# Making the rest of eight weight pieces by an adding transfer, in a hybrid decoder layer on one Trainium2 core

## The chip, the core and the metric

The kernel runs on one core of one Trainium2 chip. The metric is device time in microseconds (us): the median of the runs, beside one execution that was profiled. Five kinds of rows occur in the profile: PE is TensorE (PEld its weight loads), DVE is VectorE, ACT is ScalarE, POOL is GpSimd, SP is SyncE, which here only issues transfers. All transfers run on the core's 16 DMA engines.

## What is computed

The reference is one decoder layer in float32 with 256 tokens and a model width of 2048. Only its last line matters for the change:

```python
def swiglu(h, w_gu, w_down):
    gate, up = jnp.split(h @ w_gu, 2, axis=-1)
    return (jax.nn.silu(gate) * up) @ w_down

x = x + 0.5 * swiglu(rmsnorm(x, ffn1_norm[l]), ffn1_w_gu[l], ffn1_w_down[l])
# ... one input projection, sliding-window attention, HGRN2 recurrence, gated merge, output projection
x = x + 0.5 * swiglu(rmsnorm(x, ffn2_norm[l]), ffn2_w_gu[l], ffn2_w_down[l])
```

`w_gu` is 2048 x 11264 and `w_down` is 5632 x 2048, for either feed-forward part.

## The kernel before

**Two parts of every number.** The matrix products run in the type float32r, which keeps fewer bits than float32. So each operand is split: a first part `hi`, which is the value rounded to float32r, and a rest `lo`, which is the value less `hi`. A product of activations a and weights w is made of three: a_hi w_hi, a_hi w_lo and a_lo w_hi.

**Weights in pieces.** All weights stream from the chip's memory in 370 pieces of 1 MB (128 partitions x 2048 float32), in the order of their use; `plan` holds that order. `load_next` (line 128) issues the load of a piece into one of four buffers `w_raw`, on SP. `split_next` (line 141) makes the two parts: ACT copies `w_raw` into `w_hi`, rounding it (line 150, a CAST in the profile), and then DVE writes `w_raw - w_hi` into `w_lo` (line 151, a TENSOR_TENSOR). `w_hi` and `w_lo` have two buffers each, so the parts of piece i go where those of piece i-2 were. When `take` (line 157) hands out piece i, it issues loads up to piece i+4 and splits up to piece i+1.

**The products.** `project` (line 194) runs over the pieces of a projection. A piece holds two slices of 1024 columns (j = 0 and 1), each of two banks of 512. For each of the two token tiles and each j it issues six matmuls of 512 columns: bank 0 with hi, bank 0 with lo, bank 1 with hi, bank 1 with lo, then both banks with a_lo and hi. A piece so has 24 matmuls, of which the second is the first that reads `w_lo`. The first matmul that reads the columns 512 to 1023 of `w_lo` is the fourth, and for the next two quarters it is the eighth and the tenth.

**The second feed-forward part.** Counted from 0, the pieces 238 to 325 are those of `w_gu`: eleven groups of eight, a group being 512 gate and 512 up columns. After a group `ffn` applies silu and the product, and the result is transposed during the first two pieces of the next group: four transposes (`put_ps`) between its first and second piece, and four in the middle of the second, each followed by a CAST on ACT (`f_ah`) and a subtraction on DVE (`f_al`). The pieces 326 to 369 are those of `w_down`, 22 for either half of the columns.

**What sets the order.** The kernel is written as one sequence. The framework puts each engine's instructions in a list of its own, in an order that its scheduler chooses, and adds the waits on semaphores. Each engine runs its list in order. A transfer is issued by the engine in whose list it stands, and SP's loads are issued in order too.

Of the kernel before, what the change touches and what calls it, by code (L numbers as in the profile page):

```python
# [15 lines left out]
P = 128  # L16
D = 2048
S = 256
# [9 lines left out]
NEG = -3.0e38  # L28
# first column of each part of the input projection
C_Q, C_KV, C_GQ, C_GF, C_GI, C_GO, C_BR = 0, 1024, 1280, 2304, 3328, 4352, 5376  # L30
# places in the constants
# sums over the tokens of a chunk: from the reference, from the start, to the end, all of chunk 1 and 2
K_REF, K_HEAD, K_TAIL, K_ALL, K_SUMS = 0, 128, 256, 384, 388
K_MADD, K_TRIL, K_MLT, K_MUT, K_HM, K_INVF, K_END = 0, 128, 256, 384, 512, 640, 672
# 1 / (2 pi) in pieces of 12 bits
TURN_PIECES = 5


def turn_pieces():
    from fractions import Fraction  # L40
    import math

    # 1 / (2 pi) to 80 bits
    pi = Fraction(31415926535897932384626433832795028841971693993751, 10**49)
    rest = 1 / (2 * pi)
    out = []
    for _ in range(TURN_PIECES):
        e = math.floor(math.log2(float(rest))) - 11
        n = int(rest / Fraction(2) ** e)
        c = Fraction(n) * Fraction(2) ** e  # L50
        out.append(float(c))
        rest -= c
    return out
# [3 lines left out]
def tile_layer(  # L57
# [31 lines left out]

    # the last instruction of a kind, for others to be queued behind  # L90
    last = {}
# [3 lines left out]

# [1 line left out]
    ident = cp.tile([P, P], F32, name="ident")  # L97
# [9 lines left out]
    def load_gains(sources, c0, name):  # L107
        """vectors of P * n -> columns of gains from c0"""
        n = sum(src.shape[1] for src in sources) // P
        nat = s4(f"{name}_nat")[:n, :P]  # L110
        r = 0
        for src in sources:
            k = src.shape[1] // P
            nc.sync.dma_start(nat[r:r + k, :], src.rearrange("o (k p) -> (o k) p", p=P))
            r += k
        ps = trb(f"{name}_ps")
        transpose(ps[:, :n], nat)
        VE.tensor_copy(out=gains[:, c0:c0 + n], in_=ps[:, :n])
# [4 lines left out]

# [1 line left out]
    # The weights pass through in pieces of 1 MB, in the order of use: plan holds (name, parts), a part  # L125
    # being an access pattern and its columns in the piece.
    plan, loaded, ready = [], [], []
# [13 lines left out]
    def split_next():  # L141
        i = len(ready)
        if i < len(plan):
            raw = loaded[i]
            hi = wp.tile([P, 2048], F32R, name="w_hi", tag="hi")
            lo = wp.tile([P, 2048], F32R, name="w_lo", tag="lo")
            w = 1024 if i == 0 else 2048
            for c in range(0, 2048, w):
                c = slice(c, c + w)
                last["copy"] = SC.copy(hi[:, c], raw[:, c]).ins  # L150
                last["rest"] = VE.tensor_tensor(out=lo[:, c], in0=raw[:, c], in1=hi[:, c].bitcast(F32),  # L151
                                                op=ALU.subtract).ins
            ready.append((hi, lo))
# [12 lines left out]

    # Small work goes between the matrix products, half a piece apart.
    deferred, queues = [], []
# [25 lines left out]
    def project(name, ncols, nk, xh, xl, near_end=None):  # L194
        """(S, nk*128) @ the columns planned under name -> for each token tile its banks."""
        per = 2048 // ncols
# [4 lines left out]
        for kc in range(chunks):  # L201
            hi, lo = take(name)
            for t in range(T):
                tok = slice(t * P, (t + 1) * P)
                # the last piece bank by bank, so that they end one after the other
                order = [(range(per), [i]) for i in range(nb)] if kc == chunks - 1 else \
# [17 lines left out]
    class Normed:  # L224
        """x * gain, transposed, in two parts; the tokens' factors apart."""

# [12 lines left out]
        def add(self, q, pieces, kp):  # L239
            """columns q*512 + kp*256.. of both token tiles"""  # L240
            ps = trb(f"{self.name}_tp")
# [38 lines left out]
    class Parts:  # L280
        """transposed activations in two parts, four (128, S) tiles to a slot."""

# [10 lines left out]
        def put(self, k, n, ps, gain=None):  # L293
            """tiles k.. of a bank"""
            h, l = self.hi[k // 4], self.lo[k // 4]
# [11 lines left out]
    def put_transposed(parts, k0, nat, n, gain=None):  # L307
        """n column tiles of the token tiles nat[t] into tiles k0.. of parts"""
        for kp in range(n // 2):
            put_two(parts, k0, nat, kp, gain)  # L310
# [22 lines left out]
    def ffn(name, h, old, done):  # L333
        """done(q, pieces) takes columns q*512.. of old + ffn / 2"""
        act = Parts(f"{name}_act", 0)
# [42 lines left out]

# [1 line left out]
    wz = w_in[0]  # L380
# [8 lines left out]
    for cg in range(2):  # L389
        plan_project("po", w_out[0], cg * 1024, 1024, KT)  # L390
    plan_ffn("f2", ffn2_w_gu[0], ffn2_w_down[0])

# [1 line left out]
    xin = [[s4("xin")[:, :512] for t in range(T)] for q in range(4)]  # L394
# [15 lines left out]
    h1 = Normed("h1", "f1")  # L410
    # on both engines the activations come first
    a, v = h1.add(0, xin[0], 0)
# [5 lines left out]

    # small inputs
    pos_i = cp.tile([T, P], I32, name="pos_i")  # L420
# [13 lines left out]

    # rotary tables: gain * cos and gain * sin, tokens by 2 * 32 for queries and for keys
    rcos = cp.tile([P, T, 2, 2, 32], F32, name="rcos")
    rsin = cp.tile([P, T, 2, 2, 32], F32, name="rsin")

    def rotary_tables():
# [20 lines left out]
        def reduced(dst, src, big=1.5 * 2.0**23):  # L460
            """src less its nearest multiple of the unit at big"""
            VE.tensor_scalar(out=rd, in0=src, scalar1=big, scalar2=big, op0=ALU.add, op1=ALU.subtract)
            VE.tensor_tensor(out=dst, in0=src, in1=rd, op=ALU.subtract)
# [3 lines left out]
        for i, a in enumerate((a1.bitcast(F32), a2)):  # L467
            for j, c in enumerate(pieces):
                with tc.issue_after(last["rest"]):
                    VE.tensor_scalar(out=pr, in0=a, scalar1=c, scalar2=None, op0=ALU.mult)  # L470
                    if i == j == 0:
                        # up to 2**29: first less its multiple of 2**8
                        reduced(pr, pr, 1.5 * 2.0**31)
                    reduced(pr, pr)
                    VE.tensor_tensor(out=acc, in0=acc, in1=pr, op=ALU.add)
# [32 lines left out]

    # lower bound: the first row of the softmax over the table's two rows
    lbd = tc.dram_tile([2, HGW], F32, name="lbd")  # L510
# [29 lines left out]

# [1 line left out]
    rstd = h2.rstd  # L542
# [4 lines left out]
    def gated(name, bk):  # L547
        """silu of the banks"""
        res = []
# [18 lines left out]

# [1 line left out]
    lb, oml = s4("lb"), s4("oml")  # L570
# [10 lines left out]
    def forget():  # L581
        tiny = 2.0**-63
        for t in range(T):
# [7 lines left out]
            yield  # L591
            # log f over float32's range: f = max(f, c) * (min(f, c) / c)
            l = s4(f"logf{t}")
# [11 lines left out]
            yield  # L605
        # decay over the whole of chunks 1 and 2
        ps = trb("decay_ps")
# [15 lines left out]
    def hgrn():  # L623
        # q to the reference and to the chunk's start, k to the reference and to the chunk's end
        qs0 = [s4(f"q0{t}") for t in range(T)]
# [108 lines left out]

# [1 line left out]
    kv_bk = zproj("zkv", 256)  # L736
# [6 lines left out]
    def rotate(dst, src, t, which, nh, tmp):  # L743
        """dst, src, tmp: (P, nh, 64)"""
        c = lambda half: rcos[:, t, which, half, :].unsqueeze(1).broadcast_to([P, nh, 32])
# [11 lines left out]
    def attention():  # L757
# [25 lines left out]
        for t in range(T):  # L783
# [3 lines left out]
            VE.tensor_reduce(out=sc[:, t], in_=sq, axis=AX.X, op=ALU.add)  # L787
            # (mean + eps) ** -0.5 * HD ** -0.5
            VE.tensor_scalar(out=sc[:, t], in0=sc[:, t], scalar1=HD * EPS, scalar2=None, op0=ALU.add)
# [18 lines left out]
        def weigh(t, hq):  # L808
            """scores and their exponentials"""
            tok = slice(t * P, (t + 1) * P)  # L810
            g = hq // 2
            ss = t2("scores", (P, 4, P))
            # heads of one half of the partitions to a bank
            for e in range(2):
# [72 lines left out]

# [1 line left out]
    gA, gR = [], []  # L889
# [30 lines left out]

# [1 line left out]
    ffn("f2", h3, x2, keep(out))  # L922
# [8 lines left out]
def constants():  # L931
    """What depends on shapes alone."""
    import numpy as np
# [9 lines left out]
    sums[:, K_TAIL:K_TAIL + P] = same & (r > q)  # L943
    # per token tile two columns, for chunk 1 and for chunk 2
    sums[:, K_ALL + 0] = i >= 64
# [26 lines left out]
```

## Time and profile before

| | us |
|---|---|
| median of 3 runs | 2151.29 |
| lowest and highest | 2151.03, 2151.67 |
| span of the profiled execution, first to last instruction | 2149.6 |
| TensorE busy in it | 2139.2 |
| VectorE, ScalarE, GpSimd busy in it | 1067.7, 899.8, 14.8 |

The profiled execution has a span but no total of its own. It lies 1.7 us under the median of the runs, which is what the runs count around the first and the last instruction. A chain of waits follows the work back from the last instruction; a timeline lists one engine's instructions with start and duration.

### The profile page before, as it was taken

What the parts mean: (1) busy time and instruction counts of PE and PEld (TensorE: products, weight loads), DVE (VectorE), ACT (ScalarE), POOL (GpSimd) and SP (SyncE); (2) the same over time, 40 slices, a digit from 0 to 9 for tenths busy, and PEclk for the clock granted to TensorE, in tenths of its full rate; (3) what the DMA queues carried; (4) which work ended last, traced back from release to release, by engine and by line L of the source; (5) the groups of instructions that cost most, each with busy time, mean ns of one, the idle gap of its engine ahead of it and who ended that gap; (6) DMA issues with size and microseconds to landing.
All of it is one profiled execution on the core that took longest, in us unless ns stands there. A gap on an engine that the chain in (4) does not pass through costs nothing.

```text
span 2149.6 us, 23265 instructions
## 1 busy us (share of the span) xinstructions
PE 2139.2 (100%) x9775; PEld 1759.1 (82%) x9775; DVE 1067.7 (50%) x857; ACT 899.8 (42%) x757; POOL 14.8 (1%) x15
## 2 busy tenths in 40 slices
PE   8999999999999999999999999999999999999999
PEld 7888888888888888887777888888888888888887
DVE  4744444444444465445555565544444444444443
ACT  5543344333343354453455434444433343333332
POOL 0000000000000000000100000000000000000000
PEclk9999999999999999999999999999999999999999
DMA  7555555556565665554344555665555555565653
GB/s 275 187 195 179 194 192 184 192 192 213 194 221 189 212 208 176 178 174 137 128 164 139 186 177 189 212 201 191 196 179 194 194 183 190 191 215 192 222 198 118
DMA packets 159678, 405.87 MB, mean 189 GB/s; under 512 B 10243, under 2 KB 13014, under 8 KB 159574
## 3 DMA queue, kind: packets, MB, share of 16 engines
q1 hardware_dynamic: 156086, 398.10, 54.8%
q10 hardware_dynamic: 3488, 6.30, 0.8%
q8 instruction: 76, 1.25, 0.2%
q14 instruction: 28, 0.23, 0.0%
HBM read 398.06 MB, written 6.30 MB: 188 GB/s over the span
## 4 chain that ended last, share of the span: by engine, by line
PE 99%; DVE 0%; ACT 0%; DMA 0%; ACTq 0%; SPq 0%; issue 0%
PE f_gu L94 45%; PE f_d L94 22%; PE zbR L94 4%; PE zbA L94 4%; PE po L94 4%; PE zgo L94 2%; PE zgq L94 2%; PE zaq L94 2%; PE zgi L94 2%; PE pa L94 2%; PE zf L94 2%; PE pr L94 2%; PE put_ps L122 1%; PE o_ps L94 1%; PE s_ps L94 1%; PE zkv L94 1%
## 5 line engine op out<-in xcount | busy, mean ns | idle before, releaser
L151 DVE TENSOR_TENSOR w_lo<-w_raw,w_hi 128x2048 fp32r<-128x2048 f32 (+1 forms) x371 | 848.1, 2286 | 945.9 <-ACT w_hi L150 945.7
L150 ACT CAST w_hi<-w_raw 128x2048 fp32r<-128x2048 f32 (+1 forms) x371 | 707.3, 1907 | 1080.6 <-PE f_gu L94 501.7
L94 PE MATMUL f_gu<-w_hi,h_hi 128*128 128x512 f32 x1408 | 553.6, 394 | 2.0 <-ACT w_hi L150 2.0
L94 PE MATMUL f_gu<-w_lo,h_hi 128*128 128x512 f32 x1408 | 548.5, 390 | 0.0
L94 PE MATMUL f_gu<-w_hi,h_lo 128*128 128x512 f32 x1408 | 448.7, 390 | 0.0
L94 PEld LDWEIGHTS f_gu<-w_hi,h_hi 128*128 128x128 f32 x1408 | 265.0, 188 | 56.1 <-ACT w_hi L150 2.4
L94 PEld LDWEIGHTS f_gu<-w_hi,h_lo 128*128 128x128 f32 x1408 | 264.9, 188 | 56.0
L94 PEld LDWEIGHTS f_gu<-w_lo,h_hi 128*128 128x128 f32 x1408 | 265.0, 188 | 53.6
L94 PE MATMUL f_d<-w_hi,f_ah 128*128 128x512 f32 x704 | 274.0, 390 | 0.0
L94 PE MATMUL f_d<-w_lo,f_ah 128*128 128x512 f32 x704 | 273.6, 389 | 0.3 <-DVE w_lo L151 0.3
L94 PE MATMUL f_d<-w_hi,f_al 128*128 128x512 f32 x704 | 219.5, 389 | 0.0
L94 PEld LDWEIGHTS f_d<-w_lo,f_ah 128*128 128x128 f32 x704 | 132.1, 188 | 28.1 <-DVE w_lo L151 0.7
L94 PEld LDWEIGHTS f_d<-w_hi,f_al 128*128 128x128 f32 x704 | 132.1, 188 | 27.6
L94 PEld LDWEIGHTS f_d<-w_hi,f_ah 128*128 128x128 f32 x704 | 132.1, 188 | 27.1
L94 PE MATMUL zbR<-w_hi,h_hi 128*128 128x512 f32 x128 | 52.2, 411 | 0.0
L94 PE MATMUL zbA<-w_hi,h_hi 128*128 128x512 f32 x128 | 51.7, 407 | 0.0
L94 PE MATMUL po<-w_hi,mT_hi 128*128 128x512 f32 x128 | 50.5, 396 | 0.0
L94 PE MATMUL zbA<-w_lo,h_hi 128*128 128x512 f32 x128 | 50.0, 392 | 0.0
L94 PE MATMUL po<-w_lo,mT_hi 128*128 128x512 f32 x128 | 49.7, 390 | 0.0
L94 PE MATMUL zbR<-w_lo,h_hi 128*128 128x512 f32 x128 | 49.6, 391 | 0.0
L345 ACT ACTIVATE sg<-f_gu,h_rstd 128x512 f32<-128x512 f32 x44 | 30.2, 687 | 30.6 <-PE f_gu L94 30.4
L94 PE MATMUL zbR<-w_hi,h_lo 128*128 128x512 f32 x128 | 40.9, 391 | 0.0
(255 smaller groups left out, 1783.2 us busy)
## 6 DMA issues: line engine op xcount, KB each, us to landing
w_raw<-in_ffn_w_gu SPq DMA_DIRECT2D x352, 512.0 KB, 4.7
w_raw<-in_ffn_w_down SPq DMA_DIRECT2D x88, 1024.0 KB, 4.9
w_raw<-in_w_in SPq DMA_DIRECT2D x74, 1024.0 KB, 5.0
w_raw<-in_w_out SPq DMA_DIRECT2D x16, 1024.0 KB, 5.2
w_raw<-in_w_attn_branch SPq DMA_DIRECT2D x8, 1024.0 KB, 4.9
w_raw<-in_w_hg_branch SPq DMA_DIRECT2D x8, 1024.0 KB, 4.9
x<-old ACTq DMA_DIRECT2D x16, 256.0 KB, 5.8
old<-x SPq DMA_DIRECT2D x16, 256.0 KB, 6.1
```

Source lines behind the costliest of these rows:

```text
L94: last["mm"] = PE.matmul(o, lhsT=lhsT, rhs=rhs, start=start, stop=stop).ins
L122: PE.transpose(out=o, in_=i, identity=ident[:n, :n])
L150: last["copy"] = SC.copy(hi[:, c], raw[:, c]).ins
L151: last["rest"] = VE.tensor_tensor(out=lo[:, c], in0=raw[:, c], in1=hi[:, c].bitcast(F32), op=ALU.subtract).ins
L345: SC.activation(out=sg, in_=gt, func=AF.Silu, scale=r)
```

## The change

Eight pieces of the second feed-forward part get another split: those of number 238 or above whose number leaves 8 when divided by 16, that is 248, 264, 280, 296, 312, 328, 344 and 360. The first five are each the third piece of a group of `w_gu`; 328 is the third piece of `w_down`'s first half, 344 its nineteenth, and 360 the thirteenth of the second half. For these pieces DVE does nothing. ACT writes the negative of the raw weights into `w_lo`; since that buffer is float32r too, the value is rounded, and so is the negative of `w_hi`. Then GpSimd issues a transfer from `w_raw` to `w_lo` that adds instead of overwriting, so that `w_lo` becomes raw - hi. ACT makes `w_hi` after that, by a copy. In the pieces 264, 296, 328 and 360 negative and transfer are made in four parts of 512 columns; in 248, 280, 312 and 344 in one.

```diff
             lo = wp.tile([P, 2048], F32R, name="w_lo", tag="lo")
             w = 1024 if i == 0 else 2048
+            if i >= added_from and i % 16 == 8:
+
+                w = 512 if i % 32 == 8 else 2048
+                for c in range(0, 2048, w):
+                    c = slice(c, c + w)
+                    SC.activation(out=lo[:, c], in_=raw[:, c], func=AF.Copy, scale=-1.0)
+                    GP.dma_start(lo[:, c], raw[:, c].bitcast(F32R), accum_op=ALU.add)
+                last["copy"] = SC.copy(hi, raw).ins
+                ready.append((hi, lo))
+                return
             for c in range(0, 2048, w):
...
     for cg in range(2):
         plan_project("po", w_out[0], cg * 1024, 1024, KT)
+    added_from = len(plan)
     plan_ffn("f2", ffn2_w_gu[0], ffn2_w_down[0])
```

On ACT, at the start of the second group of `w_gu` (pieces 246 to 253; the CASTs of `w_hi` are the pieces' first parts, from piece 247 on), there stood before:

```order
L345 ACTIVATE sg<-f_gu_0_9258,h_rstd 128x512
L150 CAST w_hi<-w_raw 128x2048 x2
L300 CAST f_ah<-put_ps 128x512 x2
L150 CAST w_hi<-w_raw 128x2048 x6
L345 ACTIVATE sg<-f_gu_0_9566,h_rstd 128x512
```

and now, with the negative of piece 248 in line 153 and its first part in line 155:

```order
L355 ACTIVATE sg<-f_gu_0_9258,h_rstd 128x512
L160 CAST w_hi<-w_raw 128x2048
L153 ACTIVATE w_lo<-w_raw 128x2048
L310 CAST f_ah<-put_ps 128x512
L155 CAST w_hi<-w_raw 128x2048
L310 CAST f_ah<-put_ps 128x512
L160 CAST w_hi<-w_raw 128x2048 x6
```

The negative stands ahead of the first `f_ah`, and the first part of piece 248 has moved behind it. In the pieces cut in four, two of the four negatives stand ahead of that `f_ah` and two behind it.

On PE, at the start of piece 264 (a piece in four parts; the first `w_lo` of each bank and slice), there stood before, with the waits:

```order
L94 MATMUL f_gu_0_10118<-w_hi,h_hi 128x512 [waits Activation_49]
L94 MATMUL f_gu_0_10118<-w_lo,h_hi 128x512 [waits DVE_49]
L94 MATMUL f_gu_1_10119<-w_hi,h_hi 128x512
L94 MATMUL f_gu_1_10119<-w_lo,h_hi 128x512
L94 MATMUL f_gu_0_10118<-w_hi,h_lo 128x512
```

and now:

```order
L94 MATMUL f_gu_0_10119<-w_hi,h_hi 128x512 [waits Activation_49]
L94 MATMUL f_gu_0_10119<-w_lo,h_hi 128x512 [waits DMASW1_49]
L94 MATMUL f_gu_1_10120<-w_hi,h_hi 128x512
L94 MATMUL f_gu_1_10120<-w_lo,h_hi 128x512 [waits DMASW2_49]
L94 MATMUL f_gu_0_10119<-w_hi,h_lo 128x512
L94 MATMUL f_gu_1_10120<-w_hi,h_lo 128x512
L94 MATMUL f_gu_0_10119<-w_hi,h_hi 128x512
L94 MATMUL f_gu_0_10119<-w_lo,h_hi 128x512 [waits DMASW3_49]
L94 MATMUL f_gu_1_10120<-w_hi,h_hi 128x512
L94 MATMUL f_gu_1_10120<-w_lo,h_hi 128x512 [waits DMASW4_49]
```

The one wait for DVE has become a wait for each of the four transfers, at the matmul that first needs it. In a piece with one transfer the second matmul alone waits, and in piece 248 two matmuls with `w_hi` now stand ahead of it instead of one.

On GpSimd there was nothing in this part of the program; now there are 20 issues:

```order
L154 DMA w_lo<-w_raw 128x2048
L154 DMA w_lo<-w_raw 128x512 x4
L154 DMA w_lo<-w_raw 128x2048
L154 DMA w_lo<-w_raw 128x512 x4
L154 DMA w_lo<-w_raw 128x2048
L154 DMA w_lo<-w_raw 128x512 x4
L154 DMA w_lo<-w_raw 128x2048
L154 DMA w_lo<-w_raw 128x512 x4
```

Nothing else stands in GpSimd's list behind them. The load that next uses the `w_raw` buffer of such a piece, which waited for DVE, now waits for the transfer and for ACT's copy.

## Rows read from the trace of the kernel before

**Rows 1.** Page, busy time of the engines, share of the span, instructions.
```profile
PE 2139.2 (100%) x9775; PEld 1759.1 (82%) x9775; DVE 1067.7 (50%) x857; ACT 899.8 (42%) x757; POOL 14.8 (1%) x15
```

**Rows 2.** Page, chain that ended last, shares of the span.
```profile
PE 99%; DVE 0%; ACT 0%; DMA 0%; ACTq 0%; SPq 0%; issue 0%
```

**Rows 3.** Windows of the second feed-forward part: busy us, clock, DMA share, GB/s.
```profile
core 0: us, PE busy (x) PEld busy (x) DVE busy (x) ACT busy (x) POOL busy (x), PEclk, DMA share, GB/s
1470.00:1905.00 435.00, 435.00 (x1954) 360.08 (x1953) 204.20 (x118) 171.58 (x117) 0.00 (x0) 1.00 0.57 189
1915.00:2145.00 230.00, 230.00 (x1016) 190.42 (x1015) 99.64 (x50) 78.43 (x41) 0.00 (x0) 1.00 0.53 185
```

**Rows 4.** Chain in order of time, one group and the down part: start, us, what.
```profile
1558.37 40.85 PE f_gu L94 x180
1599.22 0.44 PE put_ps L122 x4
...
1914.26 231.26 PE f_d L94 x1020
```

**Rows 5.** Timeline of PE where piece 264 begins: start, us, instruction.
```profile
1553.89 0.39 PE L94 MATMUL f_gu<-w_lo,h_hi 128*128 128x512 f32 x1
...
1561.20 0.39 PE L94 MATMUL f_gu<-w_lo,h_hi 128*128 128x512 f32 x1
...
1563.02 0.39 PE L94 MATMUL f_gu<-w_lo,h_hi 128*128 128x512 f32 x1
```

**Rows 6.** Timeline of ACT there, with the idle time before each in brackets.
```profile
1554.77 1.91 ACT L150 CAST w_hi<-w_raw 128x2048 fp32r<-128x2048 f32 x1 [3.53 <-PE f_gu L94]
1556.58 0.58 ACT L300 CAST f_ah<-put_ps 128x512 fp32r<-128x512 f32 x1
...
1577.49 1.91 ACT L150 CAST w_hi<-w_raw 128x2048 fp32r<-128x2048 f32 x1 [3.53 <-PE f_gu L94]
```

**Rows 7.** Timeline of DVE there.
```profile
1556.71 2.29 DVE L151 TENSOR_TENSOR w_lo<-w_raw,w_hi 128x2048 fp32r<-128x2048 f32 x1 [3.14 <-ACT w_hi L150]
```

**Rows 8.** Timeline of PE around piece 344: last read two pieces back, first read.
```profile
1997.79 0.39 PE L94 MATMUL f_d<-w_lo,f_ah 128*128 128x512 f32 x1
...
2004.13 0.39 PE L94 MATMUL f_d<-w_lo,f_ah 128*128 128x512 f32 x1
```

**Rows 9.** Page, DMA issues: engine, count, KB each, median us from issue to landing.
```profile
w_raw<-in_ffn_w_gu SPq DMA_DIRECT2D x352, 512.0 KB, 4.7
w_raw<-in_ffn_w_down SPq DMA_DIRECT2D x88, 1024.0 KB, 4.9
```

**Rows 10.** DMA issues of the first 300 us, the smallest that has a time.
```profile
g_nat<-in_ffn_norm SPq DMA_DIRECT2D x2, 8.0 KB, 2.2
```

**Rows 11.** Windows at the start, where the loads run back to back.
```profile
8.00:12.00 4.00, 4.00 (x11) 3.12 (x10) 1.77 (x2) 1.56 (x2) 0.00 (x0) 1.00 1.04 388
12.00:20.00 8.00, 8.00 (x40) 6.60 (x40) 4.74 (x4) 5.05 (x7) 0.00 (x0) 1.00 1.04 385
```

**Rows 12.** Lines of POOL by shape: count, busy us, mean ns, idle before.
```profile
L790 POOL TENSOR_TENSOR a_sc<-a_sc,half_neg 128x16 f32<-128x16 f32 x2 | 6.5, 3229 | 28.4 <-DVE a_sc L789 28.4
...
L767 POOL TENSOR_TENSOR k_ms<-k_ms,half_neg 128x2 f32<-128x2 f32 x2 | 1.9, 970 | 259.9 <-DVE k_ms L766 259.9
```

**Rows 13.** Lines of ACT by shape: an operation on 512 columns of the same memory.
```profile
L237 ACT ACTIVATE junk<-old 128x512 f32<-128x512 f32 x16 | 9.9, 622 | 3.1 <-DVE old L368 1.6 <-PE f_d L94 1.5
```

**Rows 14.** Waits of SP's queue, 1470 to 1905 us: us in total, times, longest.
```profile
SPq L137 <- DVE w_lo L151: 340.2, 79, 5.1
```

**Rows 15.** Timeline of PE at the start of the kernel.
```profile
7.35 2.07 PE L94 MATMUL f_gu<-w_hi,h_hi 128*128 128x512 f32 x4 [2.04 <-ACT w_hi L150]
9.22 1.05 PE L94 MATMUL f_gu<-w_lo,h_hi 128*128 128x512 f32 x2
10.07 1.05 PE L94 MATMUL f_gu<-w_hi,h_lo 128*128 128x512 f32 x2
...
13.24 0.60 PE L122 MATMUL h_tp<-ident,xin 128*128 128x128 f32 x4
```

## Prediction

> **What bounds the kernel now.** I read the busy times first: TensorE has 2139.2 of 2149.6 us, the others at most half [rows 1]. That alone would not settle it, so the chain of waits came next: 99% of it is PE, and no other engine has a whole per cent [rows 2]. The windows of the stage that the change touches say the same more sharply: from 1470 to 1905 us and from 1915 to 2145 us PE is busy for every one of the microseconds, at the full clock of 2.4 GHz, while GpSimd does nothing and the DMA engines are busy 57% and 53% [rows 3]. The chain in order of time has nothing there but matmuls and transposes: 180 matmuls in 40.85 us, and 1020 in 231.26 us [rows 4]. That is 0.227 us each, so a piece of 24 takes 5.44 us. There is no wait in this stage that the change could take away. It can only leave PE as it is, or make it wait.
>
> So the question is how late the rest of a piece may come. In the timelines around piece 264, which stand for all eight, PE first reads `w_lo` at 1561.20 [rows 5]. ACT has made `w_hi` from 1554.77 on [rows 6], and DVE is done with the rest at 1556.71 + 2.29 = 1559.00 [rows 7]. The rest is 2.2 us early.
>
> **What the change removes and moves.** Eight subtractions of 2.29 us leave DVE [rows 7]. DVE is half idle and not on the chain, so this gains nothing. ACT gets a negative for each piece: one pass over 2048 columns costs 1.91 us as the CAST does [rows 6], four over 512 cost 0.62 each, 2.5 us [rows 13]. It is free to start sooner than the CAST did, since it needs only the buffer of the rest: the last matmul that reads `w_lo` two pieces back starts at 1553.89 and takes 0.39 [rows 5], so the negative runs from 1554.28 to 1556.19, in a stretch in which ACT had been idle for 3.53 us [rows 6]. Behind it on ACT stand `f_ah` (0.58) and the CAST of `w_hi` (1.91), done at 1558.7; the four-part form ends 0.6 later. PE needs `w_hi` one matmul ahead of 1561.20, so this is covered by some 1.7 us or more. I cost it at nothing.
>
> **What it adds: the transfer, in the place of the subtraction.** PE's second matmul of the piece now waits for it, and behind that matmul stands everything, since PE runs in order: whatever the transfer is late is added to the time. Counted from the end of the negative, it may take 1561.20 - 1556.19 = 5.0 us; in piece 248 one more matmul stands ahead, 5.2. Piece 344 has no transposes around it: the negative runs from 1997.79 + 0.39 to 2000.09 and the rest is read at 2004.13 [rows 8], so 4.0.
>
> The trace has no transfer from SBUF to SBUF, none that adds, and none that GpSimd issues. Bounds from the nearest rows: from below a plain load of the same 1 MB, 4.7 to 4.9 us from issue to landing [rows 9]. From above three terms at their worst: GpSimd takes as long to issue as its longest operation, 3.23 us [rows 12]; the fixed part is that of an 8 KB load, 2.2 us [rows 10]; and the data counts three times (raw read, old `w_lo` read, sum written). 1.05 MB at the 388 GB/s that the engines reached with the loads back to back [rows 11] is 2.7 us, so 8.1. Together 13.5 us. As the row to test this scheme on, the plain load: 2.2 + 2.7 = 4.9, as measured [rows 9].
>
> I take 1.0 us for the issue, as GpSimd's operation on two columns takes 0.97 [rows 12], 2.2 fixed, and the data twice, 5.4, since two streams must be read for one written: 8.6 us. The weight load in flight has mostly landed by then, and the next one waits for this very buffer [rows 14], so I add nothing for sharing.
>
> The Trainium skill speaks to both sides here. Its page "DMA: Bandwidth & Descriptors", section "Anatomy of one DMA - SWDGE (gpsimd) path", prices a transfer issued by GpSimd at about 2.0 us plus the bytes at 436 GB/s; the estimate from it for 1 MB is 4.4 us, and by that nothing would be late except 0.4 us in piece 344. Its page "Collectives: The Full Stack", section "The bandwidth ceiling", says that an adding transfer runs at half the rate because each sum needs two source reads; with both, the estimate is 6.8 us, and the sum would be 8 us. The 2.2 us of the 8 KB load agree with the fixed part; no run here yet shows an adding transfer.
>
> **The sum.** One transfer a piece: 8.6 - 5.2 = 3.4 for 248, 3.6 each for 280 and 312, 4.6 for 344: 15.2 us. Four transfers: the first negative is done at 1554.28 + 0.62 = 1554.9, and the data of all four follow each other, so they land at 1554.9 + 1.0 + 2.2 + 1.35 n: 1559.5, 1560.8, 1562.2 and 1563.5. They are needed at matmuls two, four, eight and ten of the piece, 1561.20, 1561.65, 1562.56 and 1563.02 [rows 5]. Only the last is late, by 0.5; in 264, 296 and 328 that is 1.5. Piece 360, like 344 without transposes, starts from 1998.18: the last lands at 2007.4 and is needed at 2005.95: 1.45. Together 3 us.
>
> The sum is 18.2 us on the profiled span of 2149.6, which is 2167.8; the runs' median lies 1.7 above the span, so 2169.5 us.
>
> **What is late next.** The load four pieces on waits for the buffer that the transfer reads, and SP's later loads queue behind it. SP already waits for these buffers, 79 times in the `w_gu` stage [rows 14]. The load for piece 268 could go at 1559.0, took 4.7 [rows 9] and was needed at 1577.49 [rows 6]: 13.8 us to spare. A transfer of 8.6 us uses some 6 of them. A transfer would have to land about 22 us after its negative before the loads cost anything.
>
> **The rivals.** *The transfer is hidden* (not slower). If it runs like a plain load, 4.7 to 4.9 us, it lands before PE asks, except by 0.9 us in piece 344; the four-part ones have landed long before. It decides at 5.0 us. For it: the load's own row, and the DMA engines are nearly half idle. Against: the fixed part alone takes 2.2, so the two reads and GpSimd's issue would have to fit in 2.8, hardly more than one pass of the data. Time: 2151 to 2152 us. The skill's plain-copy price above is this case.
>
> *The transfer is much slower.* At the upper bound of 13.5 us the one-transfer pieces are late by 8.3 + 8.5 + 8.5 + 9.5 = 34.8 us. The four-part ones are then bound by GpSimd: four issues of 3.23 in series, then 2.2 and a quarter of the data, 2.0, end 17.1 us after 1554.9, at 1572.0, 9.0 late; with 360 (10.0) 37 us. For it: GpSimd's small operations take 1 to 3 us here [rows 12]. Against: nothing in the trace. Time 2151 + 72 = 2223 us.
>
> *The clock falls in the waits.* At the kernel's start, after a wait of 2.04 us, PE's first 14 matmuls (four, and five pairs as the two shown) take 13.24 - 7.35 = 5.89 us [rows 15], 0.42 each: the pace of the lower level, 1.2 GHz, though the column of the granted clock says 1.00 there [rows 11]. At 0.227 they would have taken 3.2, so a fall costs 2.7 us. But before them PE had hardly worked at all. If each of the four long waits did the same, 10.8 us more: 2180. The Trainium skill's page "TensorE: Matmul & The Clock Gate", Part 1, has it that an idle TensorE is put back to half its clock until it has been busy again; the start agrees, and no row here shows what a wait of 3 to 5 us in the middle of full work does. With the slow transfer it would be eight falls, 21.6 us: 2245.
>
> *The negative starts late.* The buffer is freed at the matmul named above or, if the wait is coarser, with the whole piece, 0.5 us later; 4 x 0.5 plus a little for the others, 3 us, within the range.
>
> **How the numbers follow.** Waits that add up to 5 to 45 us, with or without a fallen clock: 0.67, of which the clock has 0.15. Hidden: 0.13. Much slower, above 45 us: 0.18. Faster, through nothing that I can name: 0.02. Less than 0.2%, 4.3 us, can't be told from no change. That makes faster 0.02, same 0.13, slower 0.85. The range leaves out most of the hidden case below and the end of the slow case above: 2153 to 2225.
>
> **What would show it.** In the profile after: gaps of PE at the second matmul of 248, 280, 312 and 344, ended by the transfer of `w_lo`, of 3 to 5 us; in the four-part pieces gaps under 1 us, at the tenth matmul; 8.6 us from issue to landing; negatives of 1.91 us that begin 0.5 us before the CAST did; a granted clock of 1.00; no wait for `w_raw`. Wrong would be gaps at the second matmul of a four-part piece (then GpSimd's issue, not the data, is the bound), gaps ended by ACT (then the order on ACT matters, which I cost at nothing), or no gaps.

## The result, and the profile after

The changed kernel takes 2179.0 us (median of 4 runs, 2178.43 to 2179.61) against 2151.16 in the same rounds: ratio 1.013, interval 1.0118 to 1.0142. It is slower, as forecast; 2169.5 us were predicted with a range of 2153 to 2225. The profiled span is 2177.3 us, 27.7 more than before, where the sum had 18.2.

The page after, its busy times, chain and the new queue of GpSimd's transfers (packets, MB, share of 16 engines); they answer to [rows 1, 2]:

```profile
PE 2148.0 (99%) x9775; PEld 1759.7 (81%) x9775; DVE 1050.5 (48%) x849; ACT 914.5 (42%) x777; POOL 32.7 (2%) x35
...
q0 software_dynamic: 2880, 8.39, 2.0%
...
PE 95%; DMA 3%; ACT 1%; DVE 0%; POOL 0%; SPq 0%; issue 0%; ACTq 0%
```

The chain, all PE before, now runs through transfers. In order of time (start, us, what), at piece 248 and at piece 312:

```profile
1465.68 1.92 ACT w_lo L153
1467.60 0.31 issue
1467.91 7.09 DMA w_lo<-w_raw
1475.00 0.04 issue
1475.05 37.92 PE f_gu L94 x166
...
1834.26 8.41 DMA w_lo<-w_raw
1842.66 0.04 issue
1842.71 39.26 PE f_gu L94 x166
```

From the end of the negative, 1467.60, to the landing, 1475.00, it is 7.4 us, with 5.2 to spare. The timeline of PE shows the gap in brackets, at the first matmul that reads `w_lo`. Below it are piece 264, in four parts, and 312:

```profile
1472.34 0.61 PE L94 MATMUL f_gu<-w_hi,h_hi 128*128 128x512 f32 x2
1475.05 0.73 PE L94 MATMUL f_gu<-w_lo,h_hi 128*128 128x512 f32 x2 [2.09 <-DMA w_lo<-w_raw]
...
1564.43 0.50 PE L94 MATMUL f_gu<-w_lo,h_hi 128*128 128x512 f32 x1 [0.35 <-DMA w_lo<-w_raw]
...
1565.69 0.50 PE L94 MATMUL f_gu<-w_lo,h_hi 128*128 128x512 f32 x1 [0.53 <-DMA w_lo<-w_raw]
...
1566.96 0.50 PE L94 MATMUL f_gu<-w_lo,h_hi 128*128 128x512 f32 x1
...
1568.24 0.51 PE L94 MATMUL f_gu<-w_lo,h_hi 128*128 128x512 f32 x1 [0.55 <-DMA w_lo<-w_raw]
...
1842.71 1.22 PE L94 MATMUL f_gu<-w_lo,h_hi 128*128 128x512 f32 x2 [3.38 <-DMA w_lo<-w_raw]
```

In piece 264 PE meets each of the four parts as it lands, 1.26 us apart. That is one part's 0.26 MB at 210 GB/s: the parts come one after the other at the pace of the data, but the first comes late. The brackets there add up to 1.4 us, while the piece loses 2.6: a matmul counts 0.39 us as busy where the next one normally starts after 0.227, and the one that waited is followed only after 0.34 (1564.43 to 1564.77), so each of the four stops costs some 0.28 us more than its bracket.

To say what each piece costs I take the distance between the first negatives of two successive pieces on ACT's timeline and subtract what the same distance was before: 88.98 us for two groups of `w_gu` (the chain's 44.49 each), 87.94 from 328 to 344, 87.06 from 344 to 360; for 360, the distance to the end of the span. In the changed kernel: 248: 2.4, 264: 2.6, 280: 2.5, 296: 3.0, 312: 5.0, 328: 5.4, 344: 4.3, 360: 2.2, together 27.4; 0.3 lie ahead of the first. For piece 264 these are the lines (1648.66 - 1557.04 = 91.62, less 88.98):

```profile
1557.04 1.15 ACT L153 ACTIVATE w_lo<-w_raw 128x512 fp32r<-128x512 f32 x2 [3.07 <-PE f_gu L94]
...
1648.66 1.91 ACT L153 ACTIVATE w_lo<-w_raw 128x2048 fp32r<-128x2048 f32 x1 [3.07 <-PE f_gu L94]
```

What the prediction cost at nothing cost nothing. ACT's timeline, which answers to [rows 6], has the negative at the start foretold and `w_hi` done at 1469.87, 2.5 us before PE needs it; no engine waits for `w_raw`:

```profile
1465.68 1.91 ACT L153 ACTIVATE w_lo<-w_raw 128x2048 fp32r<-128x2048 f32 x1 [3.07 <-PE f_gu L94]
1467.50 0.57 ACT L310 CAST f_ah<-put_ps 128x512 fp32r<-128x512 f32 x1
1467.96 1.91 ACT L155 CAST w_hi<-w_raw 128x2048 fp32r<-128x2048 f32 x1
```

### The profile page after: what moved, and what is told of

The parts are those of the page before. It is cut to its first block, busy times and chain, and to the rows that moved or that the text cites. A ratio compares the mean times of both kernels' runs of the same rounds, so it can differ in the third digit from the quotient of the medians.

```text
span 2177.3 us, 23341 instructions
## 1 busy us (share of the span) xinstructions
PE 2148.0 (99%) x9775; PEld 1759.7 (81%) x9775; DVE 1050.5 (48%) x849; ACT 914.5 (42%) x777; POOL 32.7 (2%) x35
## 4 chain that ended last, share of the span: by engine, by line
PE 95%; DMA 3%; ACT 1%; DVE 0%; POOL 0%; SPq 0%; issue 0%; ACTq 0%
PE f_gu L94 42%; PE f_d L94 21%; PE zbR L94 4%; PE zbA L94 4%; PE po L94 4%; DMA w_lo<-w_raw 3%; PE zgo L94 2%; PE zgq L94 2%; PE zaq L94 2%; PE zgi L94 2%; PE pa L94 2%; PE zf L94 2%; PE pr L94 2%; PE put_ps L122 1%; PE o_ps L94 1%; PE s_ps L94 1%
## 5 line engine op out<-in xcount | busy, mean ns | idle before, releaser
L161 DVE TENSOR_TENSOR w_lo<-w_raw,w_hi 128x2048 fp32r<-128x2048 f32 (+1 forms) x363 | 829.9, 2286 | 961.4 <-ACT w_hi L160 961.1
L160 ACT CAST w_hi<-w_raw 128x2048 fp32r<-128x2048 f32 (+1 forms) x363 | 692.0, 1907 | 1077.1 <-PE f_gu L94 498.9
L311 DVE TENSOR_TENSOR f_al<-put_ps,f_ah 128x512 fp32r<-128x512 f32 x44 | 28.8, 685 | 29.5 <-ACT f_ah L310 29.5
```

Source lines behind the costliest of these rows:

```text
L311: VE.tensor_tensor(out=l, in0=ps, in1=h.bitcast(F32), op=ALU.subtract)
```

## The experiments

Theory: the lateness of the transfers is the whole cost. It is made of a fixed part of some 2 us, of the data at half the rate of a load because an adding transfer reads twice, and of the weight load that shares the DMA engines. Rivals: the negatives on ACT; GpSimd's issue, four of them in series; a cost of the transfers wherever they stand. The kernels are changed from the changed kernel.

**DVE adds, in place of the transfer.**

```diff
-                    GP.dma_start(lo[:, c], raw[:, c].bitcast(F32R), accum_op=ALU.add)
+                    VE.tensor_tensor(out=lo[:, c], in0=raw[:, c], in1=lo[:, c].bitcast(F32), op=ALU.add)
```

> As the changed kernel, but in the eight pieces DVE adds the raw weights to the negative, in place of the transfer; ACT's negatives and the order on ACT stay. Theory (the transfer's lateness is the whole cost): the negative ends 5.0 us before PE reads the rest, DVE takes 2.3, so no gap of PE is left; span within 1 us of 2149.6, ratio 1.000. Rival (the negatives and the order on ACT cost something by themselves: a late w_hi, a late f_ah): gaps of PE ended by ACT stay, up to 1 us a piece, span 2153 to 2158.

2151.23 us against 2151.2, ratio 0.9999 (0.999 to 1.0009); span 2150.4, and no piece loses more than 0.1 us. The negatives and the new order on ACT are free. All of the cost is the transfer's.

**GpSimd copies, in place of adding; then ACT issues the copies.**

```diff
-                    GP.dma_start(lo[:, c], raw[:, c].bitcast(F32R), accum_op=ALU.add)
+                    GP.dma_start(lo[:, c], raw[:, c].bitcast(F32R))            # first kernel
+                    nc.scalar.dma_start(lo[:, c].bitcast(F32), raw[:, c])      # second kernel
```

> As the changed kernel, but GpSimd's 20 transfers copy the raw weights over the negative instead of adding them (so the rests of the eight pieces are the raw weights: the addition is left out). Theory (an adding transfer is bound by its two reads: 1 MB takes 5.0 us of data at 210 GB/s): the copy's data take 2.5 to 2.7 us, 1 MB lands 4.7 to 5 us after issue instead of 7.1; one-transfer pieces of w_gu lose under 0.3 us, 344 up to 1.2, the four-part ones under 0.5; span 2150 to 2153. Rival (issue by GpSimd is what is slow, not the addition): landing stays above 6.5 us and the span above 2168.

> As the run in which GpSimd copied the raw weights over the negatives (the addition is left out), but ACT issues the 20 copies, on its own queue. Theory (what issues a transfer matters little; two reads do): landing 4.4 to 5.0 us after issue as with GpSimd (4.7 to 4.9), span 2150 to 2154; issues on ACT of about 0.5 us each stand ahead of w_hi, which has 1.7 us to spare, so the four-part pieces may lose up to 0.5 us. Rival (GpSimd's issue costs a microsecond more): landing under 4.0 us.

Issued by GpSimd: 2154.21 us, ratio 1.0014 (1.0005 to 1.0024), span 2150.8. Only 328 loses more than 0.4 us (1.6). Issued by ACT: 2155.28, 1.0022 (1.0013 to 1.0032), span 2153.2; its landings lie outside the 4.4 to 5.0 us expected. The transfers in the changed kernel (count, KB each, median us from issue to landing):

```profile
w_lo<-w_raw POOLq DMA_DIRECT2D x4, 1024.0 KB, 7.2
w_lo<-w_raw POOLq DMA_DIRECT2D x16, 256.0 KB, 7.4
```

the same as copies that GpSimd issues:

```profile
w_lo<-w_raw POOLq DMA_DIRECT2D x4, 1024.0 KB, 4.9
w_lo<-w_raw POOLq DMA_DIRECT2D x16, 256.0 KB, 4.7
```

and as copies that ACT issues:

```profile
w_lo<-w_raw ACTq DMA_DIRECT2D x4, 1024.0 KB, 5.7
w_lo<-w_raw ACTq DMA_DIRECT2D x16, 256.0 KB, 5.3
```

The same transfer without the addition takes 2.3 us less, nearly one more pass of the data, and comes close to what the prediction called hidden: 3.0 us over the kernel before are left. The queue of GpSimd's transfers, which had the engines for 2.0% of the span when they added, has them for 1.1% when they copy the same bytes:

```profile
q0 software_dynamic: 2880, 8.39, 1.1%
```

So the addition is the cost. That it costs by its second read is argued from this rate; no run tells two reads from a slow adder. GpSimd's issue isn't slower than ACT's; its transfers landed sooner, which I had not expected.

**The weight load beside the transfer left out.**

```diff
+            n = len(loaded)
+            if n >= added_from + 3 and n % 16 == 11:
+                VE.memset(raw, 0.0)
+                loaded.append(raw)
+                return
             for src, n in plan[len(loaded)][1]:
```

> As the changed kernel, but the weight load that is in flight beside each of the eight transfers, that of the piece three on, is left out: DVE writes zeros into its buffer instead (eight weight pieces count as zero). Theory (the four-part pieces lose 2 to 5 us because their transfers begin beside this load and share the DMA engines with it for 2 to 3 us): first parts land 3.5 us after issue instead of 6.4, the last lands at 8.2 us after the first negative instead of 10.6, and the four-part pieces lose under 0.7 us each; the one-transfer pieces lose 1.5 to 2.5; span about 2149.6 + 12. Rival (four issues in series on GpSimd at 0.9 us, and a restart of PE at each of four waits): the four-part pieces still lose 2 us or more each; span about 2170 or more.

2167.85 us, 1.0078 (1.0061 to 1.0095). The theory holds where it was put to the test: 264 loses 0.14 us and 296 0.09, in place of 2.6 and 3.0, with the same four issues in series, and 360 loses 1.1 in place of 2.2. Of the pieces with one transfer, 248, 280 and 344 lose what they did (2.4, 3.8 and 4.2; in 280 the clock fell, as it had not before), since this load is nearly through by the time that their data start. 312 loses 2.3 in place of 5.0: its transfer lands 6.95 us after issue and not 8.41, and the clock doesn't fall there. 328 (4.7) stayed late, and in 280, 328 and 344 the clock fell, 1.6 us each, as told below; so the total came out 6 us above the 12 expected. The lines for 264, and the transfer of 312 in the chain:

```profile
1556.05 1.15 ACT L158 ACTIVATE w_lo<-w_raw 128x512 fp32r<-128x512 f32 x2 [3.07 <-PE f_gu L94]
...
1645.17 1.92 ACT L158 ACTIVATE w_lo<-w_raw 128x2048 fp32r<-128x2048 f32 x1 [3.07 <-PE f_gu L94]
...
1829.22 6.95 DMA w_lo<-w_raw
```

Windows of the changed kernel in piece 264 (last two columns: DMA share, GB/s), whose first part was issued at 1557.98:

```profile
1559.00:1560.00 1.00, 1.00 (x6) 0.82 (x5) 0.38 (x1) 1.00 (x3) 1.00 (x2) 1.00 1.02 385
...
1562.00:1563.00 1.00, 1.00 (x6) 0.81 (x5) 0.69 (x1) 0.00 (x0) 0.00 (x0) 1.00 1.12 213
...
1566.00:1567.00 1.00, 0.93 (x5) 0.42 (x3) 1.00 (x1) 0.00 (x0) 0.00 (x0) 1.00 0.21 37
1567.00:1568.00 1.00, 0.69 (x2) 0.26 (x2) 1.00 (x1) 0.00 (x0) 0.00 (x0) 1.00 0.06 10
```

and with the load left out, issued at 1556.99:

```profile
1558.00:1559.00 1.00, 1.00 (x6) 0.82 (x5) 0.40 (x1) 1.00 (x3) 1.00 (x2) 1.00 0.65 111
...
1563.00:1564.00 1.00, 1.00 (x6) 0.84 (x5) 0.00 (x0) 1.00 (x1) 0.00 (x0) 1.00 1.12 199
1564.00:1565.00 1.00, 1.00 (x6) 0.66 (x5) 0.15 (x1) 0.82 (x1) 0.00 (x0) 1.00 0.14 21
```

The GB/s tell which transfer has the engines. 385 is the pace of loads, as at the start [rows 11]; some 200 at a full DMA share is that of the adding transfer, which has two bytes to read for each that it writes. Beside the load the parts get little until about 1561; without it they begin 1.5 us after the issue and are done after 7.1, and PE works through.

**The transfers begun one piece earlier; then the same with the load beside them left out.** The negative and the transfer of piece i are issued when piece i-1 is split. `w_lo` gets a third buffer and `w_raw` gives one up.

```diff
+    def begin(i):
+        if i >= added_from and i % 16 == 8:
+            raw = loaded[i]
+            lo = begun[i] = lo_tile()    # w_lo with bufs=3; negatives and transfers as before
...
             ready.append((hi, lo))
+            begin(i + 1)
...
+            if n >= added_from + 2 and n % 16 == 10:    # second kernel alone
+                VE.memset(raw, 0.0)
```

> As the changed kernel, with the same 20 adding transfers, but begun one piece (5.44 us) earlier, into a third buffer for w_lo; to make room w_raw has three buffers instead of four, and loads are issued one piece less ahead. Theory (lateness alone): the transfers have 10 us instead of 5, the worst of them needed some 10.2 in the changed kernel, so at most the two or three worst are late by under 1 us; span 2150 to 2152, ratio 1.000 to 1.001. Rival (the transfers cost something wherever they stand, by taking the DMA engines from the weight loads): PE waits for w_raw, span above 2156.

> As the run with transfers begun one piece earlier, but the weight load that starts beside each of them, now that of the piece two on, is left out: DVE writes zeros into its buffer (eight weight pieces count as zero). Theory (begun early the transfers were still late because the load that DVE's last subtraction sets free starts with them and shares the DMA engines; 7.0 us alone against 10.4 and 11.8 beside it): the transfers land about 7 us after issue, within 0.3 us of the need; all pieces but 328 lose under 0.5 us, 328 up to 2 (loads of old stand beside it); span 2150 to 2154. Rival (something else stretches an early transfer, such as the reads of the same buffers by ACT and PE): they land after 9 us or more, span above 2160.

My expectation for the first failed: 2167.23 us, 1.0072 (1.0055 to 1.0089). Two things were wrong in it. The negative stands behind the CAST of piece i-1 on ACT, so it starts 1.81 us after that CAST instead of 4.99, 3.2 us earlier and not 5.4. And one piece earlier the transfer starts together with a load: at piece 344 GpSimd issues at 2004.58 and SP, which waits for DVE's last subtraction, at 2004.82. The second kernel tells this apart: 2151.57 us, 1.0003 (0.9994 to 1.0013); PE waits for a transfer once, 0.4 us, with all 20 adding transfers in it (line of its waits: us in total, times, longest):

```profile
PEld f_d L94 <- DMA w_lo<-w_raw: 0.4, 1, 0.4
```

Their times to landing beside the load:

```profile
w_lo<-w_raw POOLq DMA_DIRECT2D x4, 1024.0 KB, 9.5
w_lo<-w_raw POOLq DMA_DIRECT2D x16, 256.0 KB, 7.5
```

and without it:

```profile
w_lo<-w_raw POOLq DMA_DIRECT2D x4, 1024.0 KB, 7.0
w_lo<-w_raw POOLq DMA_DIRECT2D x16, 256.0 KB, 5.3
```

A load beside it costs a 1 MB adding transfer 2.5 us in the median, about the load's own 2.7 us of data. Neither the reads of these buffers by ACT and PE nor the transfers as such cost time.

**How finely to cut: one, two, four, eight parts in all eight pieces.**

```diff
-                w = 512 if i % 32 == 8 else 2048
+                w = 2048      # then 1024, 512, 256
```

> As the changed kernel, but all eight pieces get one negative and one transfer. Theory (a last part lands no earlier than the whole, as the data of all four run one after the other behind the load; and a wait of 2 to 3.5 us may let the clock fall, 1.6 us): pieces of w_gu lose 2.4 us each and 1.6 more where the clock falls, 328 some 4.5, 344 and 360 2.8 each and 1.6 with the clock; 24 to 31 us over the span of before, 2174 to 2181, no better than the changed kernel. Rival (issue in series on GpSimd is what made the four-part pieces late): 264, 296, 328 and 360 gain by having one issue, span under 2171.

> As the changed kernel, but all eight pieces are made in two parts of 1024 columns. Theory (lateness is fixed part plus data behind the load; a finer cut only starts the data sooner, up to where it meets the load, and lets PE work between the waits): pieces of w_gu lose 1 to 2.5 us, 328 some 5, 344 and 360 2 to 3, no or few falls of the clock; span between the runs with all in one (2177) and all in four (2166), 2165 to 2173. Rival (a wait costs by its count): faster than four parts, under 2165.

> As the changed kernel, but all eight pieces are made in four parts. Theory: pieces of w_gu lose 2.6 to 3.0 us each, 328 some 5.4, 344 and 360 2.1 each, and the clock does not fall, since PE works between the waits; 23 to 25 us over the span of before, 2172 to 2176, and a granted clock of 1.000. Rival (four issues in series and four restarts cost more than one long wait): slower than with one transfer in every piece, span above 2180.

> As the changed kernel, but all eight pieces are made in eight parts of 256 columns. PE waits for two of them at a time. Theory with GpSimd's issue at 0.89 us each, 7.1 us for eight, the issue takes as long as the data did: the last part is issued 6.5 us after the first negative and lands about 3.5 us later, 10 us after it where PE needs it at 8.7, so the pieces of w_gu lose 1.5 to 3 us, no better than four parts; span 2166 to 2176. Rival (an issue costs nothing where the data is the bound): the same as four parts or better, 2160 to 2166.

The second column is the median of the runs, the last is read from the profiled execution alone:

| parts | us | ratio, interval | us lost in 248, 264, 280, 296, 312, 328, 344, 360 |
|---|---|---|---|
| 1 | 2179.42 | 1.0132 (1.0115 to 1.0149) | 2.5, 3.4, 3.2, 2.5, 4.2, 5.7, 4.3, 2.8 |
| 2 | 2169.18 | 1.0085 (1.0068 to 1.0102) | 1.4, 1.7, 1.5, 1.4, 1.4, 3.8, 2.0, 2.1 |
| 4 | 2167.95 | 1.0076 (1.0061 to 1.0091) | 1.2, 2.6, 2.3, 1.2, 1.4, 4.7, 2.0, 2.2 |
| 8 | 2172.84 | 1.0100 (1.0085 to 1.0115) | 2.1, 1.7, 1.9, 2.3, 1.7, 4.5, 2.9, 3.1 |

Cutting helps, by 10 to 11 us for two or four parts, more than I expected for four (its span is 2166.5; 2172 to 2176 was written); two and four can't be told apart. With one part the clock fell in 312, 328 and 344, at 1.6 us some 5 us together; in the profiled executions with more parts it did not. That is no rule: in seven of their nine other executions the mean granted clock is 0.998 or 0.999, and the changed kernel's profiled one, with two falls, has 0.998; and with the load left out, the second part of piece 328 held PE for 2.75 us and the clock fell there too. The rest of the gain, as I read it, is that PE works on the first columns while the last are on their way. Eight parts lose some of it again; the likely reason is that GpSimd is then the pace, with eight issues in a row. In the changed kernel the four of piece 264 stand so on POOL's timeline:

```profile
1557.98 3.56 POOL L154 DMA_DIRECT2D w_lo<-w_raw  x4 [89.02 <-ACT w_lo L153]
```

and with eight parts, those of piece 312:

```profile
1830.07 7.17 POOL L154 DMA_DIRECT2D w_lo<-w_raw  x8 [84.14 <-ACT w_lo L153]
```

That is 0.89 us each: 3.6 us for four parts, less than the 5 us of their data, and 7.2 for eight, more.

**The loads of `old` left out.**

```diff
+                    if name == "f2_d":
+                        VE.memset(o, 0.0)
+                    else:
                         nc.sync.dma_start(o, old[t * P:(t + 1) * P, q * 512:(q + 1) * 512])
```

> As the changed kernel, but the loads of old (eight of 256 KB that fetch the residual of the second feed-forward part) are left out, DVE writing zeros instead; six of them stand beside the transfers of piece 328. Theory (piece 328 loses 5.4 us in the changed kernel because these loads share the DMA engines with its transfers, beside the weight load): 328 then loses 2 to 3 us like 264 and 296, the other pieces what they lost; span 2172 to 2176. Rival (the pieces of w_down are slower by themselves, by their 4 KB rows): 328 still loses 5 us.

2174.91 us, 1.011 (1.0095 to 1.0126). Piece 328 loses 1.2 us in place of 5.4, lower than expected, so its excess was these loads. The line of 344 has 9.0, because DVE's zeros had to wait for an earlier store of the same buffers and held up a later subtraction: a side effect of the edit, around 2046 us. 280 loses 4.2, as the clock fell there. 264 and 296, which the edit doesn't touch, lost 1.1 and 1.3 here and 2.6 and 3.0 before: what a four-part piece loses beside a load varies that much from run to run.

## Why the prediction was right, and which term was off

**Right: the bound, the wait and the direction.** PE was the whole chain, nothing could be gained, and the second matmul of the piece waits for the transfer. *Hidden* was wrong because of the addition, as the copies show. The Trainium skill's page "DMA: Bandwidth & Descriptors", section "Anatomy of one DMA - SWDGE (gpsimd) path", gave an estimate of 4.4 us; the copy took 4.9. The Trainium skill's page "Collectives: The Full Stack", section "The bandwidth ceiling", says it of the additions in a ReduceScatter that they need two source reads and so run at half the rate of a copy; the addition here agrees, with some 200 GB/s written against 385 to 388 for a load. *Much slower* was wrong: GpSimd's issue takes 0.9 us and not 3.2.

Of the signs that I had named, some came out otherwise. The gaps of the one-transfer pieces were 2.1 to 3.4 us, where I had 3 to 5. And a four-part piece did have a gap at its second matmul (0.35 us in 264), which was to mean that GpSimd's issue is the bound; the run without the load shows another cause. In "What is late next", the 22 us should be 17: the load can wait until 1577.49 - 4.7 = 1572.8, 16.6 us after the negative ends at 1556.19. Nothing hung on it, since no engine waits for `w_raw`.

**One transfer a piece: 15.2 us forecast, 14.2 measured.** That these are close is luck, since errors cancel. From the end of the negative to the landing I had 8.6 us; 7.4 was measured in 248. Data and fixed part were right (1.05 MB at 210 GB/s is 5.0, which leaves 2.1 of the 7.09; I had 5.4 and 2.2), but GpSimd's 0.9 us does not come on top of them; only 0.3 us pass between negative and issue. On the other side stand the late transfer of 312 (8.41 us from issue to landing) and two falls of the clock, my third rival, which had a chance of 0.15. In 312 PE waited 3.38 us, and then (windows of the changed kernel; the third column from the end is the granted clock)

```profile
1841.00:1842.00 1.00, 0.00 (x0) 0.00 (x0) 1.00 (x1) 0.00 (x0) 0.00 (x0) 1.00 0.08 16
1842.00:1843.00 1.00, 0.29 (x1) 0.29 (x2) 1.00 (x1) 0.00 (x0) 0.00 (x0) 0.56 0.00 0
1843.00:1844.00 1.00, 1.00 (x3) 0.81 (x3) 0.13 (x1) 0.00 (x0) 0.00 (x0) 0.50 0.00 0
1844.00:1845.00 1.00, 1.00 (x3) 0.71 (x3) 0.00 (x0) 0.00 (x0) 0.00 (x0) 0.50 0.87 188
1845.00:1846.00 1.00, 1.00 (x5) 0.80 (x4) 0.00 (x0) 0.00 (x0) 0.00 (x0) 0.73 1.02 391
```

it ran at 0.50, the lower of its levels, from 1842.71 until after 1845. The same happened in 344 after a wait of 2.43 us, but there PE had been working again for 1.3 us when the clock fell. The price shows in the run without the load beside, in two lines of its chain with 166 matmuls each, without and with a fall:

```profile
1474.06 37.92 PE f_gu L94 x166
...
1654.36 39.53 PE f_gu L94 x166
```

1.6 us, where I had 2.7 from the start of the kernel. In 312 of the changed kernel it was 1.3 (39.26 against 37.92 us in the chain above), as part of the fall was spent waiting. Without the two falls the term is some 11.3.

**Four transfers a piece: 3.0 us forecast, 13.2 measured.** This is the term that was mis-sized, and it is nearly the whole error of the sum. The step that failed is the sentence on sharing: "The weight load in flight has mostly landed by then, and the next one waits for this very buffer, so I add nothing for sharing." The second half is right, and for a piece with one transfer, issued 2.2 us after the negative starts, so on the whole is the first (312 is told below). But a first quarter is issued 1.3 us sooner, and the load that DVE's last subtraction sets free has then just begun. Shifted to the time of the negative in the run (1557.04 against 1554.28), I had the four landings at 1562.2, 1563.6, 1564.9 and 1566.3; PE went on with them at 1564.4, 1565.7, 1567.0 and 1568.2, each some 2 us later. With the load left out, 264 and 296 lose 0.1 us each and 360 1.1, not far from the 0.5 and 1.45 written, so the other terms of this sum held. In 328 six loads of `old` stood beside as well, 5.4 us, which I had not looked for, though SP's list has them.

**Open:** in piece 264 the engines' share is 0.06 from 1567 to 1568, while the last part is awaited. That is one of sixteen still at work, and it sets the landing. The same stands at the end of 312 (0.08 from 1841 to 1842, shown above), and in 264 with all pieces in four parts (0.05); where 264 loses 1.1 us, with the loads of `old` left out, it does not. So of the 2.6 us of 264 about half goes with this straggler, and the sharing by itself costs 1.1 to 1.4. With neither a weight load nor a load of `old` beside the transfer no such end was seen. Why one engine falls behind, and only in some executions of the same code, wasn't tried.

## What to carry to other kernels

A transfer that adds is priced here by two passes of its bytes plus some 2 us (7.1 us for 1 MB), and it competes with every load in flight when its data start; so look in the order and the timeline at what SP issues in the same 3 us, above all what the engine that is being relieved used to set free. Taking work off an engine that wasn't the bound gained nothing, and the work came back on the one path that was. If a transfer like this must be waited for, cut it in two to four: the waits then split, and PE lost its clock less often; better, begin it early enough and where no load begins.

## What the runs showed of the hardware

- An adding transfer within SBUF wrote some 200 GB/s with the engines full; 1 MB took 6.9 to 7.1 us from issue to landing with no load beside, a copy of it 4.9, beside the loads of the changed kernel.
- The clock fell after a wait of 1.91 us in one case (piece 280 without the load beside) and not after one of 3.06 (piece 264 with one transfer). In the profiled executions with all pieces in two, four or eight parts, where no wait is longer than 1.6 us, it did not fall in this stage.
- An issue of an adding transfer holds GpSimd for 0.87 to 1.05 us, whether it is for 1 MB or 128 KB.
- ACT's copies of 1 MB landed 5.7 us after issue, GpSimd's 4.9.
